# Hybrid decode step on one core: the mixers' two-operand steps moved from POOL to VectorE, copies of the inverses moved to ScalarE, two PSUM arrangements changed

## The chip, the cores and the metric

One Trainium2 chip, one of its cores. The metric is the device time of one execution in microseconds (us); the runs shown are three executions of the kernel before, and the profile is one further execution. PE is TensorE, DVE is VectorE, ACT is ScalarE, POOL is GpSimd, and SP only issues transfers (DMAs). Every engine works through its own list of instructions in the order in which the program holds them, and a waiting instruction holds up all that stand behind it on its engine.

## The reference

A decoder of two layers runs over 280 columns of tokens: 16 meta tokens and 256 prompt tokens that form one sequence of 272, and 8 single decode tokens. One layer is FFN 1, a mixing stage, FFN 2:

```python
h = x + 0.5 * swiglu(rmsnorm(x, ffn1_norm), ...)            # 1024 -> 2816 -> 1024
proj = rmsnorm(h, mix_norm) @ w_in                           # 1024 -> 2304
u_s5, p_rwkv, x_lru, g_lru = jnp.split(proj, ...)
o_s5   = s5_group_mixer(u_s5, ...)      # complex diagonal recurrence, gelu, gated
o_rwkv = rwkv7_group_mixer(p_rwkv, ...) # 6 heads of 64: S = S*w + sa (kk*a)^T + v k^T, then a norm per head
o_lru  = rglru_group_mixer(x_lru, g_lru, ...)  # conv of 4, gates, real recurrence, gelu
h = h + concat([o_s5, o_rwkv, o_lru]) @ w_out
h = h + 0.5 * swiglu(rmsnorm(h, ffn2_norm), ...)
```

Besides the outputs of all tokens, the new states of the three mixers are returned. Everything is 32-bit.

## The kernel before

Activations lie with the 1024 channels on partitions (8 tiles of 128) and the 280 tokens along the free axis. Each large product is made in three matmuls per 128 x 128 block of weights, to keep 32-bit accuracy: `wpiece` loads up to four blocks into a buffer `stg`, ACT rounds them into `whi` (L191), and an engine subtracts, `wlo = stg - whi` (L192); `gemm` then issues whi·xh, whi·xl and wlo·xh (L200 to L202). There are five `stg`, five `whi` and four `wlo` buffers. `wpiece` takes the engine of the subtraction as an argument; it is DVE unless another is named.

The mixing stage (`mixers`) of a layer has these parts:
- **Projections.** `proj` makes one tile of 128 of the 2304 channels (24 matmuls) in a PSUM bank of the kind `psa`, of which there are three; `psb` and `psc` have two each and `psd` one. `shifted` evicts it on DVE (L1300, L1304), `keys`, `decay`, `weighted` and `values` make the RWKV factors from it, `do_s` and `do_l` the inputs of the other two mixers.
- **RWKV.** The sequence is cut into a chunk of 16 and four of 64 tokens. `within` makes the matrices inside the chunks, `rwkv_inverse` inverts them (much of it on DVE, then three rounds of small matmuls with copies between, L976 to L1011), `rwkv_chunks` walks the chunks with the running state `Tc`/`st`, and `head_norm` normalises finished chunks and writes their part of `xh`/`xl`.
- **S5 and LRU.** `s5_group` (three groups of four tiles) multiplies the projections by cosines and sines, scans them on DVE (L699), rotates back and leaves `H`; `s5_close` multiplies by the output matrices and ends in `gelu2`; `s5_tail` is the gate (L756 is its matmul). `lru` is the third mixer.
- **w_out.** It is applied in two passes of eight output tiles: first the five input tiles of S5 and LRU (15 matmuls a tile, bank `psc`, 120 in all), then the three of RWKV (9 a tile, 72 in all). Each tile is added to the residual `hres` on DVE (L1509). Then `acc_sq` and `split_x` (L261, L264, L265) prepare FFN 2, whose norm factor comes back from PE at L285.

In the first w_out pass the subtraction of `wpiece` goes to POOL for two output tiles of three (`OPE = [G, G, V]`), which is 12 subtractions a layer on POOL. POOL also has the two-operand steps in the functions printed below, written `G.tensor_tensor`.

The order of instructions on each engine is not the order of the code: a list scheduler puts it together when the program is built, from its own estimates. The order is fixed from then on. Moving a step to another engine therefore moves many neighbours as well.

Of the kernel before, what the change touches and what calls it, by code (L numbers as in the profile page):

```python
# [12 lines left out]
AF = mybir.ActivationFunctionType  # L13
# [61 lines left out]
def tile_hybrid_decode(ctx, tc, *args):  # L75
# [596 lines left out]
    def s5_group(l, mp, s5, u5, u4, T, so, pc):  # L672

        ts = slice(4 * T, 4 * T + 4)
        H = mp.tile([P, 2, 4, 9 + NQ], F32, name="H", tag="H")
        G.memset(H[:, :, :, 8:9], 0.0)
        G.tensor_copy(H[:, :, :, 0:8], s5['h0'][:, :, ts])
        px = [psC()[:, :4 * (NQ + ND)].rearrange("p (a c) -> p a c", a=4) for _ in range(2)]
        for r in range(2):
            for a in range(4):  # L680
                PE.matmul(px[r][:, a], s5['xbt'][:, 4 * T + a, r], u4[:, 4 * T + a, 8:16 + NQ], start=True, stop=True)  # L681
        co, si = s5['cos'][:, ts], s5['sin'][:, ts]
        w = lambda: tmp("a", 6)[:, :4 * NQ].rearrange("p (a c) -> p a c", a=4)
        a, b, c, d = w(), w(), w(), w()

        V.tensor_tensor(a, px[0][:, :, 0:NQ], co, op=MUL)
        V.tensor_tensor(d, px[0][:, :, 0:NQ], si, op=MUL)
        V.tensor_tensor(so[0][:, ts, 1:9], px[0][:, :, NQ:], s5['lh0'][:, 0, ts], op=ADD)
        V.tensor_tensor(c, px[1][:, :, 0:NQ], co, op=MUL)
        V.tensor_tensor(b, px[1][:, :, 0:NQ], si, op=MUL)  # L690
        V.tensor_tensor(so[1][:, ts, 1:9], px[1][:, :, NQ:], s5['lh0'][:, 1, ts], op=ADD)
        G.tensor_tensor(a, a, b, op=ADD)
        G.tensor_tensor(c, c, d, op=SUB)

        S.activation(b[:, :, 1:], s5['m4'][:, ts].unsqueeze(2).to_broadcast([P, 4, NQ - 1]), AF.Copy)
        G.memset(b[:, :, 0:1], 0.0)
        fl = lambda x: x.rearrange("p a c -> p (a c)")
        for x in (a, c):
            V.tensor_tensor_scan(fl(x), fl(b), fl(x), 0.0, op0=MUL, op1=ADD)  # L699
        V.tensor_tensor(b, a, co, op=MUL)  # L700
        V.tensor_tensor(d, c, si, op=MUL)
        G.tensor_tensor(a, a, si, op=MUL)
        V.tensor_tensor(c, c, co, op=MUL)
        G.tensor_tensor(H[:, 0, :, 9:], b, d, op=SUB)
        G.tensor_tensor(H[:, 1, :, 9:], a, c, op=ADD)
        for r in range(2):
            G.tensor_copy(so[r][:, ts, 0:1], H[:, r, :, 8 + NQ:])
        return H
# [16 lines left out]
    def gelu2(out, y, q, t):  # L725

        S.activation(q, y, AF.Square)
        S.activation(q, q, AF.Copy, scale=0.044715 * SQ2PI, bias=SQ2PI)
        G.tensor_tensor(t, q, y, op=MUL)
        S.activation(t, t, AF.Tanh)  # L730
        V.scalar_tensor_tensor(out, t, 1.0, y, op0=ADD, op1=MUL)

# [30 lines left out]
    def lru(l, mp, cb, gb, s5, pc, hc, out_tile):  # L763
# [28 lines left out]
        for t in range(2):  # L792
            xc, a, r1, tx = X[t], A[t], R[t], TX[t]
            V.scalar_tensor_tensor(r1, a, 1.0, r1, op0=ADD, op1=MUL)
            G.tensor_tensor(xc, xc, r1, op=MUL)
            V.scalar_tensor_tensor(xc, tx, 1.0, xc, op0=ADD, op1=MUL)
            h = w()
            V.tensor_tensor_scan(h[:, :NPR], a[:, :NPR], xc[:, :NPR], 0.0, op0=MUL, op1=ADD)
            G.tensor_tensor(h[:, NPR:], a[:, NPR:], lr_in[:, t, 0:ND], op=MUL)
            G.tensor_tensor(h[:, NPR:], h[:, NPR:], xc[:, NPR:], op=ADD)  # L800
            G.tensor_copy(so[:, t, 0:9], h[:, NPR - 1:NPR + 8])
            gelu2(gb[:, t], gb[:, t], r1, a)
            V.scalar_tensor_tensor(gb[:, t], gb[:, t], 0.5, h, op0=MUL, op1=MUL)
            split_o(6 + t, gb[:, t])
# [101 lines left out]
    def rwkv_inverse(p0, EM):  # L906
# [59 lines left out]
        for g0, g1, bk in ((0, GRP, psB), (GRP, NU, psA)):  # L966
# [33 lines left out]
                    PE.matmul(pz[b, u], em(g0 + u)[a, h, 32:64], XN[a, g0 + u], start=True, stop=True)  # L1000
            for h in range(2):
                b = slice(64 * h + 32, 64 * h + 64)
                V.tensor_copy(Z2[b], pz[b])
            pt = bk()[:, :ng * 32].rearrange("p (u j) -> p u j", u=ng)
            for u in range(ng):
                for h in range(2):
# [1 line left out]
                    PE.matmul(pt[a, u], Z2[b, u], TT[b, g0 + u, 32:64], start=True, stop=True)  # L1008
            for h in range(2):
                a = slice(64 * h, 64 * h + 32)  # L1010
                V.tensor_copy(TT[a, us, 32:64], pt[a])  # L1011
            yield

    def rwkv_chunks(l, mp, p0, p2, inv, TT, RA, RAw, BK, BK0, EM, EO, vv, vvw, bon, xg, gu, pcl, yd, pc, decode):
# [149 lines left out]
        for c, (t0, n) in enumerate(CHUNKS):  # L1164
            if c:

                cs = slice(t0, t0 + n)
                G.tensor_tensor(RA[:, :, :, cs], RA[:, :, :, cs],
                                pcl[:, :, c - 1].unsqueeze(2).unsqueeze(3).to_broadcast([P, 3, 2, n]), op=MUL)
        for w in range(2):  # L1170
            values_by_token(w)
# [9 lines left out]
        for c, (t0, n) in enumerate(CHUNKS):  # L1181
# [19 lines left out]
            else:  # L1201
                iv = V.tensor_copy(T2, pS)
            st = p2.tile([P, 3, 64], F32, name="st", tag="st", bufs=1)
            ig = G.tensor_tensor(st, T2, pcl[:, :, c].unsqueeze(2).to_broadcast([P, 3, 64]), op=MUL)
            if out:
                outputs(*out)
            out = (c, Tc)
# [37 lines left out]
    def mixers(l, s5, acc, cols, gnext):  # L1245
# [46 lines left out]
        sho = out_tile(11, "sho")  # L1292
        dst_ = mp.tile([P, 15, ND], F32, name="dst", tag="sd")

        def shifted(i, out, ti, act=False):

            pt = proj(ti)
            pb = tmp("s", 4, p1)
            G.memset(pb[:, 0:1], 0.0)
            V.scalar_tensor_tensor(pb[:, 1:1 + NT], pt[:, :NT], KR, rs, op0=MUL, op1=MUL)  # L1300
            d = tmp("s", 4, p1)
            S.activation(d[:, 0:NPR], pb[:, 0:NPR], AF.Copy, scale=pc('rwkv_mu', i))
            S.activation(d[:, NPR:NT], sh_in[:, i, 0:ND], AF.Copy, scale=pc('rwkv_mu', i))
# [12 lines left out]
        def decay(hp):  # L1316

            hs = slice(hp * P, hp * P + P)
            pz = psB()
            PE.matmul(pz[:, :NT], lw[0:64, hs], xw[0:64], start=True, stop=True)  # L1320
            s1 = dk()
            S.activation(s1, pz[:, :NT], AF.Tanh, bias=hc('rwkv_w0', hp), scale=0.5)
            S.activation(s1, s1, AF.Copy, bias=1.0)
            pz = psB()
            PE.matmul(pz[:, :NT], lw[64:128, hs], xw[64:128], start=True, stop=True)
            at = dk()
            S.activation(at, pz[:, :NT], AF.Tanh, bias=hc('rwkv_a0', hp), scale=0.5)
# [16 lines left out]
        def keys():  # L1344
# [18 lines left out]
        def weighted(hp, kt, sq, rn, cum, pi, at, af):  # L1363
# [132 lines left out]

        acc2 = new_acc()
        n = cols.stop - cols.start
        OPE = [G, G, V]
        for kk in ([0, 1, 2, 6, 7], [3, 4, 5]):  # L1500
            rw = len(kk) == 3
            if rw:
                full[0] = True
            for j in range(KD):
                js = slice(j * P, j * P + P)
                w = wpiece([w_out[:, 3:6, js]] if rw else [w_out[:, 0:3, js], w_out[:, 6:8, js]], V if rw else OPE[j % len(OPE)])
                pt = psAB() if rw else psC()
                im = gemm(pt[:, :n], w, list(range(len(kk))), xh[:, :, cols], xl[:, :, cols], kk, True, True)
                V.tensor_tensor(hres[:, j, cols], pt[:, :n], hres[:, j, cols], op=ADD)  # L1509
# [89 lines left out]
```

## Time and profile before

| | us |
|---|---|
| three runs: median (lowest, highest) | 1263.94 (1262.67, 1265.52) |
| the profiled execution, its time | 1258.64 |
| its span, first to last instruction | 1256.8 |
| mixing stage of layer 0, from the first eviction of a projection to the first norm factor of FFN 2 | 243.7 to 441.3 |
| the same of layer 1, about | 862 to 1060 |
| busy in the span: PE, DVE, ACT, POOL | 1211.6, 971.9, 698.0, 214.4 |

How to read it: a matmul counts as busy until its modelled end, so PE's busy time overstates its work; the FFN stages are dense on PE, and the mixing stages are where DVE, ACT and POOL have long chains of small steps. The granted clock of TensorE is given as a share of its full 2.4 GHz; at 0.5 it runs at 1.2 GHz.

### The profile page before, as it was taken

How to read it: one execution, taken by the hardware profiler on the slowest of the kernel's cores; microseconds unless marked ns; L12 is line 12 of the kernel's file. 1: busy time of each engine (PE TensorE's matmuls, PEld its weight loads, DVE VectorE, ACT ScalarE, POOL GpSimd, SP SyncE). 2: the span in 40 equal slices, each digit the busy share in tenths (PEclk: the TensorE clock that was granted, in tenths of full speed). 3: DMA queues.
4: the chain of work that ended last, by engine and by line, in shares of the span. 5: the costliest groups of instructions: out<-in, count | busy, mean ns of one | idle time of the engine just before them, and what ended most of it. 6: DMA issues, size and time to landing. Idle time of an engine off the chain costs nothing.

```text
span 1256.8 us, 29154 instructions
## 1 busy us (share of the span) xinstructions
PE 1211.6 (96%) x10744; PEld 1154.9 (92%) x10744; DVE 971.9 (77%) x2345; ACT 698.0 (56%) x1529; POOL 214.4 (17%) x385
## 2 busy tenths in 40 slices
PE   7999999999898999999999999999999989999996
PEld 6999999988776999999998999998898779999996
DVE  7899957779687789985877778666876778877864
ACT  4466677564365556668544555457633656455543
POOL 2000000143443210000025000001615332500000
PEclk9999999989897999999999999999995989999998
DMA  7665654523311766554579656564423038965662
GB/s 184 170 184 161 178 145 142 164 83 107 96 29 55 187 165 183 171 170 129 155 203 240 184 169 171 171 176 128 119 79 82 2 87 226 244 196 170 190 187 83
DMA packets 376908, 187.47 MB, mean 149 GB/s; under 512 B 45532, under 2 KB 375352, under 8 KB 376766
## 3 DMA queue, kind: packets, MB, share of 16 engines
q1 hardware_dynamic: 376430, 184.47, 52.8%
q8 instruction: 84, 1.38, 0.5%
q10 hardware_dynamic: 336, 1.15, 0.3%
q14 instruction: 58, 0.48, 0.1%
HBM read 181.31 MB, written 3.37 MB: 147 GB/s over the span
## 4 chain that ended last, share of the span: by engine, by line
PE 83%; DVE 8%; DMA 4%; POOL 2%; issue 2%; ACT 1%; SPq 1%; DVEq 0%; ACTq 0%; POOLq 0%
PE psa L202 11%; PE psa L201 11%; PE psa L200 11%; PE psc L201 6%; PE psc L202 6%; PE psc L200 6%; PE psb L202 6%; PE psb L201 6%; PE psb L200 6%; PE psc L756 1%; DVE wlo L192 1%; PE psc L719 1%; PE psc L681 1%; PE psb L901 1%; DMA bc<-ds 1%
## 5 line engine op out<-in xcount | busy, mean ns | idle before, releaser
L191 ACT ACTIVATE whi<-stg 128x512 fp32r<-128x512 f32 (+2 forms) x664 | 400.7, 609 | 383.2 <-PE psa L201 101.3
L192 DVE TENSOR_TENSOR wlo<-stg,whi 128x512 fp32r<-128x512 f32 (+2 forms) x640 | 432.6, 682 | 129.2 <-ACT whi L191 29.9
L202 PE MATMUL psa<-xh,wlo 128*128 128x280 f32 (+1 forms) x930 | 274.1, 296 | 2.4 <-DVE wlo L192 2.3
L200 PE MATMUL psa<-xh,whi 128*128 128x280 f32 (+1 forms) x930 | 272.7, 294 | 2.0 <-DVE ts L1300 2.0
L201 PE MATMUL psa<-xl,whi 128*128 128x280 f32 (+1 forms) x930 | 273.0, 294 | 0.0
L202 PEld LDWEIGHTS psa<-xh,wlo 128*128 128x128 f32 x930 | 176.4, 190 | 6.0 <-DVE wlo L192 3.5
L200 PEld LDWEIGHTS psa<-xh,whi 128*128 128x128 f32 x930 | 177.1, 191 | 4.2 <-DVE ts L1300 2.2
L201 PEld LDWEIGHTS psa<-xl,whi 128*128 128x128 f32 x930 | 176.8, 190 | 1.6 <-issue 0.7
L201 PE MATMUL psc<-xl,whi 128*128 128x280 f32 (+1 forms) x498 | 144.6, 291 | 1.2 <-DVE xl L265 0.7
L202 PE MATMUL psc<-xh,wlo 128*128 128x280 f32 (+1 forms) x498 | 145.0, 291 | 0.7 <-DVE wlo L192 0.5
L200 PE MATMUL psc<-xh,whi 128*128 128x280 f32 (+1 forms) x498 | 144.8, 291 | 0.8 <-ACT xh L264 0.4
L202 PE MATMUL psb<-xh,wlo 128*128 128x280 f32 (+1 forms) x396 | 114.8, 290 | 1.0 <-DVE wlo L192 1.0
L200 PE MATMUL psb<-xh,whi 128*128 128x280 f32 (+1 forms) x396 | 115.0, 290 | 0.0
L201 PE MATMUL psb<-xl,whi 128*128 128x280 f32 (+1 forms) x396 | 114.8, 290 | 0.0
L201 PEld LDWEIGHTS psc<-xl,whi 128*128 128x128 f32 x498 | 94.0, 189 | 2.0 <-DVE xl L265 1.1
L202 PEld LDWEIGHTS psc<-xh,wlo 128*128 128x128 f32 x498 | 93.9, 188 | 1.7 <-DVE wlo L192 1.5
L200 PEld LDWEIGHTS psc<-xh,whi 128*128 128x128 f32 x498 | 93.9, 189 | 1.5 <-ACT xh L742 0.8
L202 PE MATMUL psb<-hh,wlo 128*128 128x280 f32 (+1 forms) x264 | 76.8, 291 | 0.0
L201 PE MATMUL psb<-hl,whi 128*128 128x280 f32 (+1 forms) x264 | 76.7, 291 | 0.0
L202 PE MATMUL psa<-hh,wlo 128*128 128x280 f32 (+1 forms) x264 | 76.5, 291 | 0.1
L200 PE MATMUL psb<-hh,whi 128*128 128x280 f32 (+1 forms) x264 | 76.7, 290 | 0.0
L201 PE MATMUL psa<-hl,whi 128*128 128x280 f32 (+1 forms) x264 | 76.6, 290 | 0.0
(620 smaller groups left out, 2578.7 us busy)
## 6 DMA issues: line engine op xcount, KB each, us to landing
stg<-in_ffn_w_gate_dram SPq DMA_DIRECT2D x176, 256.0 KB
stg<-in_ffn_w_up_dram SPq DMA_DIRECT2D x176, 256.0 KB
stg<-in_ffn_w_down_dram SPq DMA_DIRECT2D x160, 256.0 KB
stg<-in_w_in_dram SPq DMA_DIRECT2D x72, 256.0 KB
stg<-in_w_out_dram SPq DMA_DIRECT2D x32, 192.0 KB
bc<-ds SPq DMA_DIRECT2D x24, 192.0 KB
stg<-in_ffn_w_down_dram SPq DMA_DIRECT2D x32, 128.0 KB
bc<-ds SPq DMA_DIRECT2D x12, 256.0 KB
```

The source lines that it names most:

```text
L191: S.activation(hi[:, :kc], st[:, :kc], AF.Copy)
L192: (eng or V).tensor_tensor(lo[:, :kc], st[:, :kc], hi[:, :kc].bitcast(F32), op=SUB)
L200: PE.matmul(out, w[wk[i]][0], ah[:, k], start=(first and i == 0), stop=False)
L201: PE.matmul(out, w[wk[i]][0], al[:, k], start=False, stop=False)
L202: im = PE.matmul(out, w[wk[i]][1], ah[:, k], start=False, stop=(last and i == n - 1))
L681: PE.matmul(px[r][:, a], s5['xbt'][:, 4 * T + a, r], u4[:, 4 * T + a, 8:16 + NQ], start=True, stop=True)
L719: PE.matmul(py[32 * i:32 * i + 32, c0:c0 + n], w, x[:, o:NQ + ND], start=(m == 0), stop=(m == 2), skip_group_check=True, tile_position=(0, ...
L756: PE.matmul(pz[:, :NT], gw[k][:, j], z5[:, k, 0:NT], start=(k == 0), stop=(k == 2))
L901: PE.matmul(pg[h][:, hp], BK[r0, hp, c - 1].rearrange("p a t -> p (a t)"), RA[r0, hp, i, cs], start=True, stop=True)
```

## The change

Every two-operand step of the mixers on POOL becomes the same step on DVE, 59 a layer, and the 12 w_out subtractions follow (`OPE` is gone): 71 instructions a layer. POOL keeps fills, one-operand copies and, beside the FFNs, the update of the decode states. The two copy lines of `rwkv_inverse`, each for two halves and two groups of chunks, so eight copies a layer, go from DVE to ACT. `decay` takes its two `psb` banks at once and issues its two matmuls together. The third key projection, the fourth projection of the stage, is put into a `psc` bank.

```diff
 def s5_group(...):
-        G.tensor_tensor(a, a, b, op=ADD)
-        G.tensor_tensor(c, c, d, op=SUB)
+        V.tensor_tensor(a, a, b, op=ADD)
+        V.tensor_tensor(c, c, d, op=SUB)
...
-        G.tensor_tensor(a, a, si, op=MUL)
+        V.tensor_tensor(a, a, si, op=MUL)
         V.tensor_tensor(c, c, co, op=MUL)
-        G.tensor_tensor(H[:, 0, :, 9:], b, d, op=SUB)
-        G.tensor_tensor(H[:, 1, :, 9:], a, c, op=ADD)
+        V.tensor_tensor(H[:, 0, :, 9:], b, d, op=SUB)
+        V.tensor_tensor(H[:, 1, :, 9:], a, c, op=ADD)
...
 def gelu2(...):
-        G.tensor_tensor(t, q, y, op=MUL)
+        V.tensor_tensor(t, q, y, op=MUL)
...
 def lru(...):
-            G.tensor_tensor(xc, xc, r1, op=MUL)
+            V.tensor_tensor(xc, xc, r1, op=MUL)
...
-            G.tensor_tensor(h[:, NPR:], a[:, NPR:], lr_in[:, t, 0:ND], op=MUL)
-            G.tensor_tensor(h[:, NPR:], h[:, NPR:], xc[:, NPR:], op=ADD)
+            V.tensor_tensor(h[:, NPR:], a[:, NPR:], lr_in[:, t, 0:ND], op=MUL)
+            V.tensor_tensor(h[:, NPR:], h[:, NPR:], xc[:, NPR:], op=ADD)
...
 def rwkv_inverse(...):
-                V.tensor_copy(Z2[b], pz[b])
+                S.activation(Z2[b], pz[b], AF.Copy)
...
-                V.tensor_copy(TT[a, us, 32:64], pt[a])
+                S.activation(TT[a, us, 32:64], pt[a], AF.Copy)
...
 def rwkv_chunks(...):
-                G.tensor_tensor(RA[:, :, :, cs], RA[:, :, :, cs],
+                V.tensor_tensor(RA[:, :, :, cs], RA[:, :, :, cs],
...
-            ig = G.tensor_tensor(st, T2, pcl[:, :, c].unsqueeze(2).to_broadcast([P, 3, 64]), op=MUL)
+            ig = V.tensor_tensor(st, T2, pcl[:, :, c].unsqueeze(2).to_broadcast([P, 3, 64]), op=MUL)
...
 def decay(hp):
-            pz = psB()
+            pz, pa = psB(), psB()
             PE.matmul(pz[:, :NT], lw[0:64, hs], xw[0:64], start=True, stop=True)
+            PE.matmul(pa[:, :NT], lw[64:128, hs], xw[64:128], start=True, stop=True)
...
 def keys():
-                shifted(3 + hp, kt[hp], 6 + hp)
+                shifted(3 + hp, kt[hp], 6 + hp, bank=psC if hp == 2 else psA)
...
 def weighted(...):
-            G.tensor_tensor(ka, kn, at, op=MUL)
+            V.tensor_tensor(ka, kn, at, op=MUL)
...
-                G.tensor_tensor(BK[r0, hp, :, h], by_c(kt)[r0], by_c(pi)[r0], op=MUL)
-            G.tensor_tensor(BK0[:, hp, 1], kt[:, :16], pi[:, :16], op=MUL)
+                V.tensor_tensor(BK[r0, hp, :, h], by_c(kt)[r0], by_c(pi)[r0], op=MUL)
+            V.tensor_tensor(BK0[:, hp, 1], kt[:, :16], pi[:, :16], op=MUL)
...
 def values(...):
-            G.tensor_tensor(RA[:, hp, 1], rt[:, :NPR], pp[:, :NPR], op=MUL)
+            V.tensor_tensor(RA[:, hp, 1], rt[:, :NPR], pp[:, :NPR], op=MUL)
...   (three more of the same kind)
 # w_out
-        OPE = [G, G, V]
...
-                w = wpiece([w_out[:, 3:6, js]] if rw else [w_out[:, 0:3, js], w_out[:, 6:8, js]], V if rw else OPE[j % len(OPE)])
+                w = wpiece([w_out[:, 3:6, js]] if rw else [w_out[:, 0:3, js], w_out[:, 6:8, js]])
```

What the scheduler makes of it is seen at three places of layer 0 (layer 1 has the same pattern).

PE at the end of the mixing stage, before: the last gate matmuls (L756) and transposes of `head_norm` (L175, L177), then the first w_out pass (L200 to L202 into `psc`).

```order
L756 MATMUL psc<-u_3941,gw 128x280 x5
L175 MATMUL psa<-ident,EM 64x64
L177 MATMUL psa<-ident,EM 64x64
...
L200 MATMUL psc<-xh,whi 128x280
L201 MATMUL psc<-xl,whi 128x280
L202 MATMUL psc<-xh,wlo 128x280
```

The same place now:

```order
L756 MATMUL psc<-u_3941,gw 128x280 x3
L200 MATMUL psc<-xh,whi 128x280
L201 MATMUL psc<-xl,whi 128x280
L202 MATMUL psc<-xh,wlo 128x280
...
L175 MATMUL psa<-ident,EM 64x16
L177 MATMUL psa<-ident,EM 64x16
```

Before, all transposes of the three head norms stand ahead of the 120 matmuls of the first w_out pass. Now 30 of the 120 stand ahead of the first head norm's transposes, and the other 90 ahead of those of the second and third.

DVE where the first S5 group is scanned (L699) and rotated back (L700 to L705), before:

```order
L688 TENSOR_TENSOR sore<-psc,lh_1065 128x4x8
L699 SCALAR_TENSOR_TENSOR ta<-ta 128x272 x2
L1003 COPY Z_4848<-psb 32x96 x2
L992 COPY TT<-psb 16x3x16
L1202 COPY Tc<-psd 128x192
L700 TENSOR_TENSOR ta<-ta,cs 128x272
L701 TENSOR_TENSOR ta<-ta,cs 128x272
L1011 COPY TT<-psb 32x3x32 x2
L703 TENSOR_TENSOR ta<-ta,cs 128x272
```

The same place now:

```order
L699 SCALAR_TENSOR_TENSOR ta<-ta 128x272
L960 STREAM_TRANSPOSE TT<-wk 128x16x2x16
L699 SCALAR_TENSOR_TENSOR ta<-ta 128x272
L959 STREAM_TRANSPOSE AD<-wk 128x16x2x16
L700 TENSOR_TENSOR ta<-ta,cs 128x272
L701 TENSOR_TENSOR ta<-ta,cs 128x272
L702 TENSOR_TENSOR ta<-ta,cs 128x272
L703 TENSOR_TENSOR ta<-ta,cs 128x272
L704 TENSOR_TENSOR H<-ta 128x4x68
L976 COPY Zs<-psb 128x48
L705 TENSOR_TENSOR H<-ta 128x4x68
```

The rotation now runs through on DVE, ahead of the rounds of the inverse (L976 onwards), and it stands among the last steps of the inverse's DVE part (L959, L960), which before were finished earlier.

DVE inside that DVE part of the inverse (L941, L943), now; before, no subtraction of a w_out piece stood there, the first ones were on POOL:

```order
L941 TENSOR_TENSOR wk<-DD,XI 128x16
L904 TENSOR_TENSOR EO<-psc,emask 128x3x64
L941 TENSOR_TENSOR wk<-DD,XI 128x16
L943 TENSOR_TENSOR zz<-wk 128x16
L192 TENSOR_TENSOR wlo<-stg,whi 128x384
L941 TENSOR_TENSOR wk<-XI,zz 128x16 x2
L192 TENSOR_TENSOR wlo<-stg,whi 128x256
```

The first two w_out pieces are now subtracted on DVE between steps of the inverse, so that the inverse stands behind their transfers.

## Rows read from the trace of the kernel before

**Rows 1.** The page: busy time by engine, and the chain by engine.

```profile
PE 1211.6 (96%) x10744; PEld 1154.9 (92%) x10744; DVE 971.9 (77%) x2345; ACT 698.0 (56%) x1529; POOL 214.4 (17%) x385
...
PE 83%; DVE 8%; DMA 4%; POOL 2%; issue 2%; ACT 1%; SPq 1%; DVEq 0%; ACTq 0%; POOLq 0%
```

**Rows 2.** Busy time in stretches: length, engines' busy us, PE's clock, DMA.

```profile
243.70:321.00 77.30, 74.63 (x581) 66.48 (x581) 62.90 (x148) 43.26 (x113) 28.14 (x62) 0.96 0.34 93
321.00:332.00 11.00, 10.77 (x176) 8.52 (x176) 3.85 (x13) 6.90 (x22) 4.39 (x8) 1.00 0.41 119
332.00:401.50 69.50, 59.45 (x1053) 45.91 (x1051) 57.75 (x166) 36.14 (x94) 30.16 (x49) 0.78 0.18 46
401.50:441.30 39.80, 39.80 (x308) 39.21 (x309) 27.47 (x66) 22.92 (x49) 9.95 (x12) 1.00 0.69 180
...
950.00:1020.00 70.00, 63.12 (x1064) 50.37 (x1063) 55.88 (x160) 35.54 (x92) 28.50 (x47) 0.73 0.14 37
```

**Rows 3.** POOL's groups by shape, 238 to 445 us: count, busy us, mean ns.

```profile
L192 POOL TENSOR_TENSOR wlo<-stg,whi 128x384 fp32r<-128x384 f32 x6 | 6.2, 1035 | 24.7 <-ACT whi L191 22.5 <-PE psc L202 2.2
...
L702 POOL TENSOR_TENSOR ta<-ta,cs 128x272 f32<-128x272 f32 x3 | 2.7, 911 | 4.6 <-DVE ta L700 4.6
```

**Rows 4.** DVE's groups by shape, 238 to 445 us.

```profile
L192 DVE TENSOR_TENSOR wlo<-stg,whi 128x512 fp32r<-128x512 f32 x44 | 31.5, 722 | 7.1 <-PE psa L202 3.2 <-ACT whi L191 1.8 <-PE psb L202 1.5
L192 DVE TENSOR_TENSOR wlo<-stg,whi 128x384 fp32r<-128x384 f32 x10 | 5.5, 552 | 3.0 <-PE psc L202 2.0 <-ACT whi L191 1.0
...
L1379 DVE TENSOR_TENSOR BK<-ta,tg 64x256 f32<-64x256 f32 x6 | 3.4, 567 | 0.0
...
L1381 DVE TENSOR_TENSOR tf<-tg,tf 128x280 f32<-128x280 f32 x3 | 2.5, 826 | 0.0
...
L703 DVE TENSOR_TENSOR ta<-ta,cs 128x272 f32<-128x272 f32 x3 | 2.1, 707 | 0.1
...
L1380 DVE TENSOR_TENSOR BK<-ta,tg 128x16 f32<-128x16 f32 x3 | 1.9, 620 | 0.1
...
L1200 DVE TENSOR_TENSOR Tc<-psb,st 128x192 f32<-128x192 f32 x4 | 1.4, 347 | 0.1
...
L700 DVE TENSOR_TENSOR ta<-ta,cs 128x272 f32<-128x272 f32 x3 | 1.3, 437 | 0.1
L690 DVE TENSOR_TENSOR ta<-psc,cs 128x272 f32<-128x272 f32 x3 | 1.3, 429 | 0.0
...
L1003 DVE COPY Z<-psa 32x288 f32<-32x288 f32 x2 | 0.9, 458 | 0.0
...
L192 DVE TENSOR_TENSOR wlo<-stg,whi 128x256 fp32r<-128x256 f32 x2 | 0.8, 414 | 0.0
...
L1003 DVE COPY Z<-psb 32x96 f32<-32x96 f32 x2 | 0.5, 257 | 0.0
```

**Rows 5.** DVE's groups by shape, 80 to 200 us, where POOL is idle.

```profile
L192 DVE TENSOR_TENSOR wlo<-stg,whi 128x512 fp32r<-128x512 f32 x72 | 48.8, 683 | 15.9 <-PE psd L627 4.8 <-PE psb L202 3.9 <-ACT whi L191 3.2
...
L384 DVE SCALAR_TENSOR_TENSOR smex<-smex,smex 128x12 f32<-128x12 f32 x15 | 2.4, 160 | 0.0
```

**Rows 6.** Timeline, two DVE steps: start us, duration us.

```profile
325.17 0.44 DVE L686 TENSOR_TENSOR ta<-psc,cs 128x272 f32<-128x272 f32 x1 [1.09 <-PE psc L681]
325.53 0.43 DVE L687 TENSOR_TENSOR ta<-psc,cs 128x272 f32<-128x272 f32 x1
```

**Rows 7.** Waits, 241 to 420 us: total us, times, longest us.

```profile
DVE ts L1300 <- PE psa L202: 5.8, 4, 3.9
...
DVE gb L1446 <- PE psa L202: 2.3, 1, 2.3
```

**Rows 8.** SP's timeline, then the chain: u restacked, gate weights, first w_out piece.

```profile
310.49 10.46 SPq L670 DMA_DIRECT2D u<-u  x16
321.04 1.99 SPq L749 DMA_DIRECT2D gw<-in_s_glu_w_dram  x3
...
323.13 3.30 DMA stg<-in_w_out_dram
```

More of the change, by code (lines that the diff above doesn't have):

```diff
@@ L1261, in out_tile, with proj @@
             return t
-        def proj(i):
+        def proj(i, bank=psA):
             w = wpiece(w_in[:, :, i * P:i * P + P])
-            pt = psA()
+            pt = bank()
             gemm(pt[:, :NT], w, ks, xh, xl, ks, True, True)
@@ L1293, in mixers, with shifted @@
         dst_ = mp.tile([P, 15, ND], F32, name="dst", tag="sd")
-        def shifted(i, out, ti, act=False):
-            pt = proj(ti)
+        def shifted(i, out, ti, act=False, bank=psA):
+            pt = proj(ti, bank)
             pb = tmp("s", 4, p1)
@@ L1323, in decay @@
             S.activation(s1, s1, AF.Copy, bias=1.0)
-            pz = psB()
-            PE.matmul(pz[:, :NT], lw[64:128, hs], xw[64:128], start=True, stop=True)
             at = dk()
-            S.activation(at, pz[:, :NT], AF.Tanh, bias=hc('rwkv_a0', hp), scale=0.5)
+            S.activation(at, pa[:, :NT], AF.Tanh, bias=hc('rwkv_a0', hp), scale=0.5)
             af = dk()
@@ L1392, in values @@
             shifted(hp, rt, 3 + hp, True)
-            G.tensor_tensor(RA[:, hp, 1], rt[:, :NPR], pp[:, :NPR], op=MUL)
+            V.tensor_tensor(RA[:, hp, 1], rt[:, :NPR], pp[:, :NPR], op=MUL)
             w, kv = dst_[:, 5 * hp + 1:5 * hp + 3, 0:ND], dst_[:, 5 * hp + 3:5 * hp + 5, 0:ND]
-            G.tensor_tensor(w[:, 0], w[:, 1], rt[:, NPR:NT], op=MUL)
-            G.tensor_tensor(dots[:, hp], kv, rt[:, NPR:NT].unsqueeze(1).to_broadcast([P, 2, ND]), op=MUL)
+            V.tensor_tensor(w[:, 0], w[:, 1], rt[:, NPR:NT], op=MUL)
+            V.tensor_tensor(dots[:, hp], kv, rt[:, NPR:NT].unsqueeze(1).to_broadcast([P, 2, ND]), op=MUL)
             decode_start(mp, ds, dst_, hp)
             S.activation(rt, rt, AF.Copy, scale=pc('rwkv_r_k', hp))
-            G.tensor_tensor(rt, rt, kt, op=MUL)
+            V.tensor_tensor(rt, rt, kt, op=MUL)
             shifted(6 + hp, vv[:, hp], 9 + hp, True)
```

## The prediction

> **What bounds the kernel now.** I read the page first. PE is busy for 96% of the span and carries 83% of the chain that ended last, POOL 2% of it, which is 25 us [rows 1]. So POOL's own time is worth little by this view. But a matmul's busy time is modelled, so I cut layer 0's mixing stage into stretches instead [rows 2]. Only there does POOL have the steps that move. Three things are to be seen.
>
> From 401.5 to 441.3, PE is busy for all 39.8 us, at full clock, with 308 matmuls: 0.129 us each. This is the real PE bound. It holds the whole first w_out pass (120 matmuls, 15.5 us), the second (72, 9.3 us), and the start of FFN 2.
>
> From 332.0 to 401.5, where the RWKV chunks and the S5 groups run, DVE is busy for 57.75 of 69.5 us: 11.75 us of gaps. PE's 59.45 us there are mostly the modelled ends of small matmuls, and its clock is granted at 0.78 on average, that is at 1.2 GHz for nearly half of the stretch. Layer 1 is alike: 950 to 1020 has DVE at 55.9 of 70 us and a clock of 0.73. So this part is set by DVE and by chains through DVE, and a PE job that could run here is free.
>
> From 243.7 to 321.0, the projections, DVE is busy for 62.9 of 77.3 us; its largest named waits are for projections on PE, 5.8 us in four waits, the longest 3.9, and 2.3 us for the last one (`gb`) [rows 7]. From 321 to 332 DVE is busy for only 3.85 of 11 us.
>
> **The change, term by term, for one layer.** All prices are in DVE's busy time. Two steps of 0.44 us start 0.36 us apart [rows 6], so one in a run costs its duration less 0.08.
>
> *Added to DVE: 71 steps.* 31 have 272 or 280 elements (three each of L1375, L1393, L1399, five for each of three S5 groups, five gelu steps, two in the LRU); such a step with two SBUF inputs lasts 0.437 us (L700) on DVE and 0.911 on POOL (L702) [rows 3, 4]: 31 × 0.36 = 11.2. Four of 384 elements (L1168) and six subtractions of 384 at 0.552: 10 × 0.47 = 4.7. Six subtractions of 256 and six BK steps (64 x 256) at 0.414: 12 × 0.33 = 4.0. Five state steps of 192 at 0.347: 5 × 0.27 = 1.3. Thirteen tiny ones: a small step lasts 0.160 [rows 5], so 0.08 to 0.16 each, I take 0.1: 1.3. Sum 22.5 us: 6 of it in the projections (three each of L1375, L1393, L1399, six BK steps, nine tiny ones: 3.2 + 2.0 + 0.9), 16.5 after.
>
> *Taken from DVE: eight copies.* Those of 288 columns last 0.458 us, their small brothers at most that [rows 4]; four large at 0.38 and four small at half of it or so: 2.3 us. On ACT they hide: it is busy for 36.1 of 69.5 us [rows 2].
>
> *Relief.* The trace shows DVE steps drawn out where POOL works. The same form of step lasts 0.437 at L700, 0.707 at L703 and 0.826 at L1381; BK at L1379 0.567 against 0.414 for 256 elements; a 16-element step 0.620 at L1380 [rows 4]; the large subtraction 0.722 against 0.683 where POOL is idle [rows 4, 5]. With their counts: 0.8 + 1.2 + 0.9 + 1.4 + 44 × 0.039 = 1.7, together 6.0 us. A step with one input in PSUM (L690, 0.429) is not drawn out. I take 6, four of it in the projections. Below, it is 0 (if the long steps are long for another reason); above, 12, if steps that never met an idle POOL hide as much again. The Trainium skill says why, in "SBUF — State Buffer", section "Who interferes with whom": a VectorE instruction with two SBUF inputs and a GpSimd instruction that reads SBUF exclude each other, one with fewer SBUF inputs does not. By that rule all of the excess goes, and the trace agrees (0.707 against 0.429).
>
> *Net.* DVE's load in the stage rises by 22.5 − 2.3 − 6.0 = 14 us. With an unchanged order this would be the end of the story, and a bad one. The order is what changes.
>
> *The end of the stage.* Of the 120 first-pass matmuls none ran before the last head norm's transposes; now all 120 stand ahead of those of the second and third head norm. They leave the dense part and go into the stretch in which PE idles. What stays behind the last `xl` of the head norm is 39.8 − 15.5 = 24.3 us. DVE then has still nine adds to `hres`, eight `split_x`, seven `acc_sq` and some nine subtractions, about 15 us, against 9.3 of second-pass matmuls, so the first tile of FFN 2 waits for the last of its inputs; much of that tile can run before. I add 2: 26.3.
>
> *The stretch from 321 to 401.5 (80.5 us).* DVE busy 3.85 + 57.75 = 61.6; added 16.5; copies −2.3; relief −2; and drawn in from the dense part seven adds and eight subtractions: 7 × 0.36 + 6 × 0.47 + 2 × 0.33 = 6.0. Sum 79.8. The gaps were 7.15 + 11.75 = 18.9. The first 7.15 lay behind the last projection; in the new order DVE has the rest of the inverse, the S5 products and the state scaling in that place, so I leave 2. Of the 11.75, part was DVE waiting for S5 steps that went to POOL and back; these now follow each other on DVE. I leave 6. Neither figure is measured: the bounds are 0 and 18.9. New length 87.8.
>
> *The projections (77.3 us).* DVE +6 − 4 of relief; the fourth projection no longer waits for a `psa` bank, and DVE gets it without the 3.9 us wait, of which I count 3; the 2.3 before `gb` is filled, since `gb` now stands among other work. Length 74.0. The pair in `decay` is counted at nothing: its two matmuls only swap places with projections.
>
> *Sum.* 74.0 + 87.8 + 26.3 = 188.1 against 197.6 (243.7 to 441.3): −9.5 us a layer, −19 for both. That is made against the span of 1256.8 of the profiled execution, whose time is 1258.6; the median of the runs is 5.3 above that, and I carry the difference over unchanged: 1263.9 − 19 = 1245.
>
> **The rivals.** The bound for telling a difference from none is 0.2%, 2.5 us.
>
> *R1, slower: VectorE's own waits stay.* The instructions come from POOL into an engine that works in order; a step that waits (for PE in the inverse, for ACT in gelu) now holds up all else. Place: 321 to 401.5. If all 18.9 us of gaps stay, the stretch takes 98.7 and the stage 199.0, +1.4 a layer or 1267; every further us of waiting adds 2 to the time. It decides from gaps of 17.5 us on. Against it: the long gap behind the last projection has new work in it. For it: 79.8 us of work in an 80 us stretch is a full engine. Three such us give 1273. The Trainium skill's "Perfetto Trace Analysis", section "Optimizing Scalar/DVE Operations", speaks for this rival: from a saturated VectorE, some work may well go to ScalarE or even GpSimd, it says (with the reservation that VectorE and GpSimd share a port), and the change does the reverse. No run here shows yet which of the two weighs more.
>
> *R2, half the gain is lost to the w_out pieces.* The first of them now stands on DVE inside the inverse. Its transfer is issued behind 16 restacking transfers, which need 10.46 us after the last S5 projection is evicted, then 2 us of gate weights, and lands 3.3 us later [rows 8]; with ACT's rounding about 16.5 us. If DVE gets there in 12, it and the whole inverse wait 4.5 us: −5 a layer, 1254. Against it: PE has still four projections to make meanwhile, 96 matmuls or 12.4 us, and DVE waits for `gb` ahead of that place.
>
> *R3, more gain.* The gaps close to 3 us, and relief is 12: −9.5 − 5 − 6 is the floor, chains through PE will keep some of it; I take −16 a layer, 1232. The low clock of the end of the stage would go too, since the 120 matmuls then keep PE at work there.
>
> *R4, no change.* The added 14 us of load eat the 15.5: within 2.5 us of 1264.
>
> **How the numbers follow.** Forecast (1238 to 1252) 0.50; R2 (1252 to 1261) 0.17; R3 0.14; R4 0.08; R1 0.11. The likeliest gives 1245. Its own range is 1238 to 1252, from gaps of 5 to 11.5 us. The range that leaves out R1 and half of R3 is 1233 to 1262. Faster by over 0.2%: the first three, 0.81; within: 0.08; slower: 0.11.
>
> **What would show it.** Right: POOL nearly empty in the mixing stages; L703 and L1381 at 0.44; the distance from the first projection's eviction to FFN 2's first norm factor near 188 instead of 197.6; first-pass w_out matmuls ahead of the last head-norm transposes in time; DVE busy over 90% from the last projection to the last `xl`. Wrong: gaps on DVE before its new neighbours (R1), a DVE wait for `whi` in the inverse (R2), or the first tile of FFN 2 waiting for `split_x` by more than 2 us.

## The result and the profile after

The changed kernel is slower: 1281.72 us (median of 4; 1277.12 to 1283.38) against 1263.31 for the kernel before, run beside it, a ratio of 1.0152 (95% interval 1.0127 to 1.0178). The profiled execution took 1277.12 us. The ratios below are those on record; they differ from the ratios of the medians by up to 0.2%.

The page of the changed kernel, busy time and chain by engine:

```profile
PE 1219.6 (96%) x10744; PEld 1162.9 (91%) x10744; DVE 985.2 (77%) x2471; ACT 702.3 (55%) x1545; POOL 106.4 (8%) x243
...
PE 82%; DVE 8%; DMA 4%; ACT 3%; issue 1%; SPq 0%; DVEq 0%; ACTq 0%
```

Against [rows 1], POOL lost half of its work and DVE gained only 13.3 us. From the first L285 of the mixing stage to that of FFN 2, layer 0 takes 210.0 us against 198.5 before, layer 1 203.1 against 201.4. The three stretches of layer 0 that the prediction used (columns as in [rows 2]), then the middle one of layer 1:

```profile
247.60:320.60 73.00, 72.52 (x574) 63.51 (x574) 56.77 (x164) 42.61 (x114) 8.82 (x33) 0.94 0.40 110
320.60:427.20 106.60, 91.12 (x1312) 75.72 (x1311) 79.97 (x240) 51.53 (x135) 6.54 (x22) 0.74 0.20 56
427.20:455.30 28.10, 28.10 (x200) 27.51 (x201) 19.88 (x50) 14.99 (x32) 2.98 (x4) 0.92 0.56 142
950.00:1053.00 103.00, 88.82 (x1311) 73.67 (x1310) 79.26 (x239) 51.05 (x134) 5.46 (x20) 0.75 0.20 55
```

Projections 73.0 us (predicted 74.0), dense part 28.1 (26.3), DVE's work in the middle 80.0 (79.8): all near. But the middle lasts 106.6 us where 87.8 were predicted, because DVE stands still in it for 26.6 us instead of 8; in layer 1 for 23.7 of 103.0. These gaps, 18.6 and 15.7 us more than forecast, are in size nearly all of the 37 us between forecast and result. In layer 1 they were there before too: the same stretch (937.0 to 1022.6) had 25.0 us of them, so there the change filled hardly any, and DVE's added work made the stretch longer.

What DVE does in the front of that stretch, from its timeline (start, duration, idle time before and what ended it):

```profile
324.32 0.44 DVE L686 TENSOR_TENSOR ta<-psc,cs 128x272 f32<-128x272 f32 x1 [0.89 <-PE psc L681]
...
325.12 1.08 DVE L947 TENSOR_TENSOR wk<-XI,zz 128x512 f32<-128x512 f32 x1
...
328.29 0.44 DVE L686 TENSOR_TENSOR ta<-psc,cs 128x272 f32<-128x272 f32 x1 [0.35 <-PE psc L681]
...
330.65 0.72 DVE L699 TENSOR_TENSOR_SCAN ta<-ta 128x272 f32<-128x272 f32 x1
331.29 1.01 DVE L960 STREAM_TRANSPOSE TT<-wk 128x512 f32<-128x512 f32 x1
332.16 0.66 DVE L699 TENSOR_TENSOR_SCAN ta<-ta 128x272 f32<-128x272 f32 x1
332.74 1.02 DVE L959 STREAM_TRANSPOSE AD<-wk 128x512 f32<-128x512 f32 x1
...
343.70 0.36 DVE L1202 COPY Tc<-psd 128x192 f32<-128x192 f32 x1 [0.97 <-PE psd L1197]
344.09 0.36 DVE L1204 TENSOR_TENSOR st<-Tc,pcl 128x192 f32<-128x192 f32 x1
348.01 1.23 DVE L829 TENSOR_TENSOR bc<-bc,sd 128x1024 f32<-128x1024 f32 x1 [3.56 <-DMA sd<-in_state_rwkv_dram]
...
368.47 0.44 DVE L704 TENSOR_TENSOR H<-ta 128x272 f32<-128x272 f32 x1 [2.17 <-PE psc L719]
```

The first S5 groups (L686 to L699) stand between the last steps of the RWKV inverse (L947 to L960), two of them with waits for PE of 0.89 and 0.35 us, and the inverse stands behind those waits and behind S5's own work. The decode state's transfer holds the whole engine for 3.56 us. At L704, DVE waits 2.17 us for matmuls that still read the old `H`; that wait was POOL's before.

At the end of the stage RWKV is held up a second time. Its last chunk output is written at 395.91 us. PE then has all 120 matmuls of the first w_out pass ahead of the last head norm's transposes, and in DVE's list the steps of the last two head norms (L1116, L1119) stand among the adds and subtractions of that pass. ACT, DVE and PE there:

```profile
395.91 0.33 ACT L1158 ACTIVATE EM<-psb 128x192 f32<-128x192 f32 x1 [0.91 <-PE psb L1155]
...
416.95 0.34 DVE L1116 TENSOR_REDUCE smyv<-EM 128x3 f32<-128x192 f32 x1
...
420.66 0.29 PE L202 MATMUL psc<-xh,wlo 128*128 128x280 f32 x1
420.88 0.24 PE L175 MATMUL psa<-ident,EM 64*64 64x64 f32 x1
...
424.05 0.24 PE L175 MATMUL psa<-ident,EM 64*64 64x64 f32 x1 [1.82 <-DVE EM L1119]
...
427.17 0.38 DVE L1137 TENSOR_TENSOR xl<-bon,xh 128x216 fp32r<-128x216 f32 x1 [0.45 <-ACT xh L1136]
```

From the last chunk output to RWKV's last `xl` it takes 31.3 us; in the kernel `a_noB` of the experiments, where no matmul of the first pass stands ahead, 11.0.

### The profile page after: what moved, and what is told of

Read it like the earlier page. It is cut to its first block, busy times and chain, and to the rows that moved or that the text cites. A ratio compares the mean times of both kernels' runs of the same rounds, so it can differ in the third digit from the quotient of the medians.

```text
span 1275.4 us, 29148 instructions
## 1 busy us (share of the span) xinstructions
PE 1219.6 (96%) x10744; PEld 1162.9 (91%) x10744; DVE 985.2 (77%) x2471; ACT 702.3 (55%) x1545; POOL 106.4 (8%) x243
## 4 chain that ended last, share of the span: by engine, by line
PE 82%; DVE 8%; DMA 4%; ACT 3%; issue 1%; SPq 0%; DVEq 0%; ACTq 0%
PE psa L202 11%; PE psa L201 11%; PE psa L200 11%; PE psc L201 6%; PE psc L200 6%; PE psc L202 6%; PE psb L202 6%; PE psb L201 6%; PE psb L200 6%; DMA stg<-in_ffn_w_gate_dram 2%; PE psc L681 1%; PE psb L901 1%; DVE wlo L192 1%; PE psa L177 1%; DMA stg<-in_ffn_w_up_dram 1%
## 5 line engine op out<-in xcount | busy, mean ns | idle before, releaser
L192 DVE TENSOR_TENSOR wlo<-stg,whi 128x512 fp32r<-128x512 f32 (+2 forms) x664 | 440.8, 671 | 136.4 <-ACT whi L191 31.8
L202 PE MATMUL psa<-xh,wlo 128*128 128x280 f32 (+1 forms) x914 | 267.8, 294 | 2.6 <-DVE wlo L192 2.6
L200 PE MATMUL psa<-xh,whi 128*128 128x280 f32 (+1 forms) x914 | 268.0, 294 | 2.4 <-DVE ts L1300 2.4
L201 PE MATMUL psa<-xl,whi 128*128 128x280 f32 (+1 forms) x914 | 268.2, 294 | 0.0
L202 PEld LDWEIGHTS psa<-xh,wlo 128*128 128x128 f32 x914 | 173.0, 190 | 6.1 <-DVE wlo L192 3.9
L200 PEld LDWEIGHTS psa<-xh,whi 128*128 128x128 f32 x914 | 173.9, 191 | 4.2 <-DVE ts L1300 2.9
L200 PE MATMUL psc<-xh,whi 128*128 128x280 f32 (+1 forms) x514 | 152.0, 296 | 3.9 <-ACT xh L1136 3.2
L201 PE MATMUL psc<-xl,whi 128*128 128x280 f32 (+1 forms) x514 | 151.3, 294 | 1.9 <-DVE xl L743 1.1
L202 PE MATMUL psc<-xh,wlo 128*128 128x280 f32 (+1 forms) x514 | 151.3, 294 | 0.9 <-DVE wlo L192 0.7
L202 PE MATMUL psb<-xh,wlo 128*128 128x280 f32 (+1 forms) x396 | 114.7, 290 | 0.7 <-DVE wlo L192 0.7
L200 PE MATMUL psb<-xh,whi 128*128 128x280 f32 (+1 forms) x396 | 115.2, 291 | 0.0
L200 PEld LDWEIGHTS psc<-xh,whi 128*128 128x128 f32 x514 | 98.8, 193 | 5.3 <-ACT xh L1136 3.6
L201 PEld LDWEIGHTS psc<-xl,whi 128*128 128x128 f32 x514 | 98.6, 192 | 3.1 <-DVE xl L743 2.0
L202 PEld LDWEIGHTS psc<-xh,wlo 128*128 128x128 f32 x514 | 98.5, 192 | 2.1 <-DVE wlo L192 2.0
L202 PE MATMUL psb<-hh,wlo 128*128 128x280 f32 (+1 forms) x264 | 76.8, 291 | 0.0
L202 PE MATMUL psa<-hh,wlo 128*128 128x280 f32 (+1 forms) x264 | 76.5, 291 | 0.1
L200 PE MATMUL psb<-hh,whi 128*128 128x280 f32 (+1 forms) x264 | 76.6, 290 | 0.0
```

Source lines behind the costliest of these rows:

```text
L192: (eng or V).tensor_tensor(lo[:, :kc], st[:, :kc], hi[:, :kc].bitcast(F32), op=SUB)
L200: PE.matmul(out, w[wk[i]][0], ah[:, k], start=(first and i == 0), stop=False)
L201: PE.matmul(out, w[wk[i]][0], al[:, k], start=False, stop=False)
L202: im = PE.matmul(out, w[wk[i]][1], ah[:, k], start=False, stop=(last and i == n - 1))
```

## The experiments

Four marks are used, in us after the first L285 matmul of the mixing stage: the inverse's end, the last subtraction into `xl` by a head norm ("RWKV") and by S5 or LRU, and the last add to `hres`. "b" kernels start from before, "a" kernels from the changed one. Layer 0, one profile each:

| kernel | ratio to before, 95% | inverse | RWKV | S5 | last add |
|---|---|---|---|---|---|
| before | 1 | 109.7 | 159.1 | 158.8 | 183.9 |
| changed | 1.0152 (1.0127, 1.0178) | 121.9 | 182.2 | 156.3 | 195.7 |
| b_S | 0.9968 (0.9942, 0.9994) | 115.4 | 171.3 | 148.2 | 181.9 |
| b_P | 0.9894 (0.9863, 0.9925) | 111.7 | 164.3 | 152.3 | 180.5 |
| b_O | 0.9955 (0.9937, 0.9973) | 116.3 | 164.0 | 159.5 | 185.5 |
| b_C | 0.9990 (0.9966, 1.0014) | 110.8 | 159.9 | 159.6 | 184.7 |
| b_SPCO | 1.0010 (0.9982, 1.0039) | 117.8 | 176.7 | 155.6 | 188.8 |
| b_I | 0.9979 (0.9954, 1.0004) | 112.1 | 160.7 | 159.2 | 184.4 |
| b_D | 0.9974 (0.9954, 0.9995) | 113.4 | 166.3 | 166.0 | 191.1 |
| b_B | 1.0032 (1.0012, 1.0051) | 115.3 | 167.1 | 160.7 | 187.3 |
| b_DB | 1.0041 (1.0011, 1.0071) | 115.1 | 167.2 | 160.8 | 187.6 |
| b_PCI | 0.9898 (0.9865, 0.9932) | 107.5 | 155.4 | 155.1 | 180.2 |
| b_PCI_Sg | 0.9915 (0.9889, 0.9941) | 113.3 | 167.4 | 151.8 | 181.1 |
| b_PCI_Sl | 0.9909 (0.9880, 0.9938) | 111.7 | 162.4 | 160.9 | 186.2 |
| a_noI | 1.0132 (1.0090, 1.0174) | 124.1 | 179.8 | 161.6 | 190.4 |
| a_noS | 1.0067 (1.0040, 1.0094) | 115.2 | 173.0 | 153.4 | 186.4 |
| a_noB | 0.9947 (0.9923, 0.9971) | 104.7 | 150.0 | 153.8 | 178.9 |
| a_noBS | 0.9899 (0.9861, 0.9936) | 106.3 | 160.8 | 149.9 | 176.6 |
| a_Bq | 1.0058 (1.0033, 1.0084) | 113.2 | 171.1 | 146.5 | 183.6 |
| a_q | 1.0049 (1.0028, 1.0070) | 108.5 | 158.7 | 158.4 | 183.5 |

One execution's marks can be some us off its median: b_D's profile took 1266.0 us, the slowest of its ten, whose median is 1259.98, and a_Bq's 1257.08 us, the fastest of its ten, whose median is 1267.45.

**The four groups of moved steps, each alone.** The edits are the lines of the change, cut into S (`s5_group`, `gelu2`, `lru`), P (`weighted`, `values`), O (w_out subtractions), C (chunk steps). For C:

```diff
-                G.tensor_tensor(RA[:, :, :, cs], ...
+                V.tensor_tensor(RA[:, :, :, cs], ...
-            ig = G.tensor_tensor(st, T2, ...
+            ig = V.tensor_tensor(st, T2, ...
```

> The kernel before with the S5, gelu and LRU steps alone on VectorE (26 a layer). Theory A (the RWKV chain: the moved steps stand in VectorE's list between the steps of the inverse and of the chunk states, so the last state step L1200 of layer 0, 130.5 us after the norm factor L285 before and 149.9 in the changed kernel, comes late): this part carries most of the loss; L1200 at 140 or later, time 1270 to 1280. Theory B (the w_out pieces: their subtractions inside the inverse wait for transfers, and 90 first-pass matmuls stand ahead of two head norms): L1200 at 130 to 133, time 1258 to 1264.

> The kernel before with the two-operand steps of weighted and values alone on VectorE (33 a layer, 21 of them small or in the projections' shadow). Theory A: VectorE reaches the last within-chunk product L904 (69.0 us after L285 before, 77.2 in the changed kernel) 4 to 8 us later, and the stage grows by half of that, 1266 to 1270. Theory B: no loss here, and the steps beside it get shorter (L1379, L1380, L1381, together 3 us a layer), 1258 to 1264.

> The kernel before with the w_out subtractions alone on VectorE (12 a layer). Theory B: this is the loss; the first-pass matmuls move ahead of the head norms, the two waits for wlo inside the inverse (2.9 and 2.0 us) appear, 1272 to 1280. Theory A: the S5 steps stay off VectorE, its list holds few steps between those of the chain, L1200 stays within 3 us of 130.5, time 1258 to 1266.

> The kernel before with the chunk steps alone on VectorE (L1168 and the state scaling, 9 a layer). These lie on the RWKV chain itself: the scaling takes 0.64 us on GpSimd and 0.35 on VectorE, and its hand-over between engines goes. Theory A: the chain gets 1 to 3 us shorter, time 1258 to 1263. Theory B says nothing against that: the same.

Medians 1257.84, 1250.37, 1257.88 and 1261.78 us against 1262.48: each alone is faster or even, b_P by more than either theory allowed. As the cause of the loss by itself, theory A fell, and of theory B the part on the w_out pieces. A's mechanism was there, though: with S, RWKV ends 12 us later, only S5 ends 10 us earlier. B's other part was not tried by b_O, which in layer 0 puts only 12 of the 120 first-pass matmuls ahead of the last head norm; b_S puts 105 there, the changed kernel all 120.

**The moves together, and the rest alone.** b_SPCO has all 71 moved steps and nothing else, b_I the copies on ACT, b_DB the two PSUM edits, a_noI the change without the copies.

```diff
-                V.tensor_copy(Z2[b], pz[b])                      # b_I
+                S.activation(Z2[b], pz[b], AF.Copy)
```

> The kernel before with all 71 two-operand steps on VectorE, and nothing else: the inverse copies stay on VectorE, decay and the banks as before. The four parts alone gave -4.6, -12.1, -4.6 and -0.7 us. Theory C (the rest of the change, copies or banks, costs what was lost): the parts add up in the main, 1238 to 1250. Theory D (together they fill VectorE's list, and the RWKV chain waits in it): 1272 to 1282, last L1200 of layer 0 near 150 us after L285.

> The kernel before with the eight inverse copies on ScalarE alone. Theory C in its first form (the copies wait in ScalarE's list, the inverse gets longer): 1268 to 1280, the distance from the first L976 to the last L1011, 28.0 us in layer 0 before, 31 or more. Theory D and the second form of C: 1258 to 1266.

> The kernel before with the two PSUM arrangements alone (decay's pair, the fourth projection's bank). Theory C in its second form (the fourth projection stands ahead of the norm factor's matmuls L285 and delays them, 2.7 us in the changed kernel, and the decay pair holds both psb banks): 1268 to 1280, L904 last at 73 us or more after L285 (69.0 before). Theory D and the first form of C: 1258 to 1266.

> The changed kernel with the eight inverse copies back on VectorE. First form of C: 1238 to 1255. Second form of C and theory D: 1275 to 1285.

1262.20, 1261.44, 1268.32 and 1279.18 us against 1261.39. b_SPCO lies between the ranges of C and D. Both halves hold a part of the cause: four gains of 4.6, 12.1, 4.6 and 0.7 us add up to nothing, and the PSUM edits cost 5 us by the ratio, 7 by the medians. The copies are innocent.

From these profiles came theory E: w_out's last add is at the later of S5 + 25 and RWKV + 13. The first w_out pass needs S5's `xl` and the second, shorter one needs RWKV's. Over the two layers of all 20 kernels this gives the last add to within −2.4 and +3.2 us. Before, S5 decides (183.8) and RWKV has 12 us to spare. Each group alone spends some of them (P 5, S 12, O 5, C 1) and pays nothing or next to nothing; together they make RWKV 17.6 us later, and it decides. By this rule that is why the gains do not add. The two marks are not independent, however: in both layers of the changed kernel, b_SPCO, a_noS and a_Bq all 120 first-pass matmuls, which need S5, stand ahead of the last head norm, and RWKV's mark comes 3 to 8 us after the last of them.

**Which PSUM edit; theory E tried.** b_D has decay's pair alone, b_B the fourth projection's bank alone, a_noS the change with S back on POOL, b_PCI the groups P and C with the copies.

```diff
-                shifted(3 + hp, kt[hp], 6 + hp)                  # b_B
+                shifted(3 + hp, kt[hp], 6 + hp, bank=psC if hp == 2 else psA)
```

> The kernel before with decay's pair alone. The two arrangements together cost 5 us, and in their trace the decay scans come 2.0 and 3.9 us later, the last L904 5.1 us later. Theory F (the loss is the pair: both psb banks are held until two activations have read them): 1265 to 1270, L904 last 71 us or more after L285. Theory G (the loss is the fourth projection, put ahead of the norm factor's matmuls): within 2 us of before.

> The kernel before with the fourth projection's bank alone. Theory G: 1265 to 1270, the first eviction L1300 at 2.2 us after L285 instead of 1.5, L285 itself 2 to 3 us late, decay scans late by 2. Theory F: within 2 us of before.

> The changed kernel with the S5, gelu and LRU steps back on GpSimd. Theory E (two chains meet in w_out: its last add comes at the later of S5's last xl + 25 us and RWKV's last xl + 13 us; S5 steps on VectorE shorten the first chain by 8 to 10 and lengthen the second by as much): RWKV's last xl of layer 0 falls from 181 to 170 to 174 us after L285, S5's goes from 156 to 160 to 166, time 1264 to 1272. Theory H (VectorE's load as such, with which each of the four parts adds its share): 26 steps less a layer, but they gained 4.6 us alone, so 1278 to 1284.

> The kernel before with the steps of weighted and values, the chunk steps and the inverse copies in their new places; S5, LRU, w_out, decay and banks as before. Theory E: the parts that do not lengthen the RWKV chain much (P 161.9 us after L285, C and I as before) add up: 1243 to 1250, RWKV's last xl at 158 to 164, S5's at 152 to 158. Theory H: no better than P alone, 1250 to 1258.

1259.98, 1265.51, 1271.87 and 1250.71 us against 1261.62. It is the bank (G), not the pair. a_noS is 8 to 11 us better than the full change (by medians and by ratios, each against its own kernel before), its RWKV mark fell to 173.0 as E has it. b_PCI is no better than P alone in time (H's figure, at the edge of E's).

The bank's direct cost stands in PE's timeline, first of before, then of the changed kernel:

```profile
242.29 0.29 PE L202 MATMUL psa<-xh,wlo 128*128 128x280 f32 x1
242.64 0.68 PE L285 MATMUL psd<-ident,nrm 128*128 128x128 f32 x4
```

```profile
245.23 0.29 PE L202 MATMUL psc<-xh,wlo 128*128 128x280 f32 x1
245.36 0.93 PE L285 MATMUL psd<-ident,nrm 128*128 128x128 f32 x6
```

DVE finishes the norm factor in both at 242.5 to 242.7. With a bank free, PE's list holds 21 of the fourth projection's 24 matmuls ahead of L285, and the factor, for which every eviction of the stage waits, comes 2.7 us later.

**The bank inside the changed kernel, and what E can foretell.** a_noB is the change without the bank, a_noBS also without S. b_PCI_Sg and b_PCI_Sl add the S5 group steps, or the gelu and LRU steps, to b_PCI.

> The changed kernel with the fourth projection back in a psa bank, all else as changed. Theory E (two chains): L904 last falls from 77 to 72 us after L285, RWKV's last xl from 182 to about 176, the stage starts 2.5 us earlier; time 1256 to 1266. If the bank costs no more here than alone (4 us): 1276 to 1279.

> The changed kernel without the bank and with the S5, gelu and LRU steps on GpSimd. Theory E: RWKV's last xl at 160 to 168, S5's at 152 to 158, last w_out add at 177 to 182; time 1244 to 1254. Theory H (every moved step adds load): 1258 to 1266.

> b_PCI (1250.7) with the five S5 group steps on VectorE too (15 a layer). In b_PCI S5 ends at 155.1, RWKV at 155.4, so w_out is bound by S5 + 25 = 180, RWKV has 12 us to spare. Theory E: S5 4 to 8 earlier, RWKV 4 to 8 later, last add at 173 to 178, time 1238 to 1247. Theory H: 1252 to 1260.

> b_PCI (1250.7) with the gelu and LRU steps on VectorE too (11 a layer, 5 of them gelu products on the S5 chain). Theory E: S5 3 to 6 earlier, RWKV 2 to 5 later, last add at 174 to 178, time 1238 to 1247. Theory H: 1252 to 1258.

1255.11, 1245.11, 1250.18 and 1250.83 us against 1260.59. One line makes about 25 us (24 by medians, 26 by ratios): without the bank the change is faster than before. The size was not foreseen: a_noB's RWKV mark came at 150.0, not at about 176. a_noBS has the lowest median seen, with a ratio level with those of b_P and b_PCI; its S5 mark and last add came earlier than forecast. The last two missed: the rule says what the two marks make of the end, not how a new order will set the marks (Sl's S5 came at 160.9 in layer 0 and 152.9 in layer 1).

The middle stretch of a_noB, `gb`'s eviction to the last `xl`, and what follows:

```profile
317.80:397.00 79.20, 66.19 (x1206) 50.37 (x1205) 68.26 (x208) 45.00 (x122) 7.72 (x22) 0.89 0.15 40
397.00:436.70 39.70, 39.70 (x307) 39.11 (x308) 30.77 (x73) 23.05 (x49) 2.99 (x4) 1.00 0.69 180
```

DVE's gaps are 10.9 us here, near the 8 of the forecast, and PE's clock is at 0.89 instead of 0.74.

**Place or order.** a_Bq keeps the bank but queues the fourth projection's matmuls behind L285. a_q keeps bank and place, and queues the first S5 group's DVE steps behind the inverse's last transposition. `issue_after` puts what it holds behind an instruction in that engine's list, without a wait; `RM[0]` is the last L285 matmul, `LAST['it']` the transposition.

```diff
+                with (tc.issue_after(RM[0].ins) if hp == 2 else ExitStack()):     # a_Bq
+                    shifted(3 + hp, kt[hp], 6 + hp, bank=psC if hp == 2 else psA)
...
+        with tc.issue_after(LAST['it'].ins):                                      # a_q
+            R['0'] = s5_group(l, R['p2'], s5, u5, R['u4'], 0, so, pc)
```

> The changed kernel; only PE's matmuls of the fourth projection are queued behind those of the norm factor (L285), the psc bank stays. Theory J (the place ahead of L285 is what costs, by 2.7 us at L285 and what follows from it): L285 of layer 0 back at 242 to 244, RWKV's last xl at 150 to 165 us, time 1248 to 1260. Theory K (the bank itself, or the mere shift of the later order, costs): 1270 to 1284.

> The changed kernel; only the first S5 group's VectorE steps are queued behind the inverse's last transposition on VectorE. In the changed kernel eight of them, 3.3 us, and a scan stand ahead of it, and the inverse ends 121.9 us after L285, against 104.7 without the bank. Theory L (that order is most of the 17 us): inverse ends at 106 to 114, RWKV's last xl at 160 to 172, time 1260 to 1270. Theory M (it is the 5 us later start and slow PE stretches, not this order): inverse ends at 116 or later, 1274 to 1284.

1267.45 and 1264.93 us against 1259.79. a_q takes back about 13 us by order alone (1.0049 against 1.0152, each to the kernel before that was run beside it; the medians themselves differ by 17): same work, same engines, the same late norm factor. DVE in it, at the place shown above:

```profile
319.94 1.08 DVE L949 TENSOR_TENSOR wk<-XI,zz 128x512 f32<-128x512 f32 x1
321.06 0.69 DVE L951 TENSOR_REDUCE XI<-wk 128x64 f32<-128x512 f32 x1
...
323.00 1.04 DVE L962 STREAM_TRANSPOSE TT<-wk 128x512 f32<-128x512 f32 x1
323.89 1.02 DVE L961 STREAM_TRANSPOSE AD<-wk 128x512 f32<-128x512 f32 x1
324.74 0.43 DVE L686 TENSOR_TENSOR ta<-psc,cs 128x272 f32<-128x272 f32 x1
```

(Lines from the inverse on are 2 or 3 higher there.) From the last large product (L947, here L949) to the second transposition's start it now takes 3.95 us, against 7.62 (325.12 to 332.74). The inverse ends at 108.5 instead of 121.9 and RWKV at 158.7 instead of 182.2. So the forecast of theory L came out near, but not through that place alone. Of the 23.5 us at RWKV's mark, 8.8 are there when the second transposition ends, 4.6 more come in the rounds up to the inverse's end, and 10.1 behind it. The scheduler had rebuilt the order at the end of the stage too: 1 first-pass matmul (layer 1: 12) stands ahead of the last head norm in a_q, none in a_noB, all 120 in the changed kernel. Both runs undo both hold-ups in the main, and no run moves the head norms alone; how the loss divides between them is not shown.

a_Bq lies between J and K: the norm factor is back at 242.4 and about 12 us are won by the ratio, but some S5 steps still stand inside the inverse (113.2) and all 120 matmuls ahead of the last head norm.

## Why the prediction was wrong, point by point

- **"I leave 2. ... I leave 6": the step that failed.** DVE's gaps in the middle stretch were 26.6 us. R1 named the mechanism (a waiting step holds up all behind it), but priced it at 1267 to 1273 with a chance of 0.11. Without the bank edit the gaps are 10.9 us: what kept them open was the order that this edit brought about. The prediction also left out PE's clock: in layer 0 the granted clock in the stretch fell from 0.81 (the two parts of [rows 2] weighted by length) to 0.74, and the 48 matmuls of L681 took 421 ns in the median instead of 275. In layer 1 it did not fall (0.72 before, 0.75 after), and no run separates the clock's share from the order's.
- **"The fourth projection no longer waits for a psa bank ... of which I count 3": wrong in sign.** The wait was there, but PE's order was not read up to L285. Direct cost 2.7 us at the factor in layer 0; inside the changed kernel about 25 us, together with S5 steps inside the inverse and the first pass ahead of the head norms, of which a_noB has only three S5 steps there, without a wait, and none of the pass. That the later start brings these about is an argument: in a_Bq the factor is on time and both are still there.
- **The first w_out pass leaving the dense part.** It did (28.1 left, predicted 26.3), but won nothing: its first add stayed put (402.8 before, 403.5 after), since it needs S5's last `xl`. It ran instead ahead of two head norms, whose steps waited behind it on PE and DVE, so RWKV's last `xl` came later. The prediction counted this move as gain alone and gave the head norms' wait no price. In a_noB the pass is back behind the chains (39.7), and the kernel is faster all the same. I weighed the stretch by DVE's load where two chains and their meeting decide.
- **Added load and relief.** By the page DVE gained 6.7 us a layer, predicted 14. With additions of 22.5 and 2.3 for the copies as estimated, the relief is 13.5, over the upper bound of 12. The slow forms of [rows 4] have all become normal:

```profile
L1379 DVE TENSOR_TENSOR BK<-ta,tg 64x256 f32<-64x256 f32 x6 | 2.5, 416 | 0.0
...
L1381 DVE TENSOR_TENSOR tf<-tg,tf 128x280 f32<-128x280 f32 x3 | 1.3, 444 | 0.0
...
L703 DVE TENSOR_TENSOR ta<-ta,cs 128x272 f32<-128x272 f32 x3 | 1.3, 439 | 0.0
...
L1380 DVE TENSOR_TENSOR BK<-ta,tg 128x16 f32<-128x16 f32 x3 | 0.5, 177 | 0.0
```

  The Trainium skill, "SBUF — State Buffer", section "Who interferes with whom", says that a two-input VectorE step and a GpSimd step reading SBUF shut each other out; by that rule all of the excess goes, and the trace agrees (826 to 444 ns).
- **Decay's pair at nothing, copies hidden on ACT:** right; alone they gave ratios of 0.9974 and 0.9979.
- **R2** happened in part: DVE waits 2.0 us for `whi` inside layer 0's inverse, against 4.5 us in R2. The wait of 2.9 us that b_O's expectation puts there as well stands at 262.88 us, before a projection's piece and 45 us ahead of the inverse. O alone was 4.6 us faster than before.

## What to carry to other kernels

Where two chains meet, write down which decides and how many us the other has to spare: edits that each spend part of that slack look free alone and are not together. Before a bank or buffer is made free, read what the work it frees will stand in front of; a matmul early in the list can delay a factor for which everything waits. In an in-order engine, an added step costs its wait as well as its duration, so move steps of the other chain last, and pin the order where it matters.

## What the runs showed of the hardware

The relief of VectorE by idle POOL, 13.5 us a layer with the added work as estimated, was twice the 6.0 that the visible slow forms suggested: a 16-element step went from 620 to 177 ns. Executions of one program on one chip spread by up to 1.5% (1242.62 to 1260.89 us for b_PCI), so the differences of 1 to 3 us between single parts above are not to be read one by one.
